# A casting transfer of GpSimd's in place of ScalarE's rounding, for the weight blocks of the second group's input projections

## The chip, the core and the metric

The kernel runs on one NeuronCore of a Trainium2 chip. Its engines are TensorE (PE in the profile; PEld is its weight load), VectorE (DVE), ScalarE (ACT), GpSimd (POOL) and SyncE (SP), which only issues transfers. Each has its own queue, worked off in order, and they meet at semaphores. The metric is the device time of one execution in microseconds (us); lower is better.

## What is computed

One layer of an encoder that mixes three groups of heads: a state-space scan in both directions (SSD), banded window attention, and cross-attention to a memory. It is applied to two requests with the same weights, 1024 rows and 256 rows, of width 2048, all in float32. Cut to what matters:

```
def layer(x, mem, ...):
    hn = rms_norm(x, norm_g)
    proj = hn @ w_in
    xbc, z_ssd, dt_raw, q, k, v, z_att, mq, z_mem = split_cols(proj, IN_SIZES)
    ...                       # convolution, scan, window attention, memory attention, gates
    return x + concatenate([o_ssd, o_att, o_mem], axis=-1) @ w_out
```

The two large products, by w_in and by w_out, are most of the arithmetic.

## The kernel before

The 1280 rows are ten tiles of 128; the kernel works in two groups of five tiles (640 rows). A float32 product is made of three products of float32r numbers, a form with fewer bits: each operand is split into a rounded part (h) and the rest (l = raw - h), and TensorE adds xH·wh, xH·wl and xL·wh in PSUM.

**The split of the weights.** The weights come in blocks of 128 x 512 (256 KB; those of kv are 128 x 288, 144 KB). SyncE loads a block into `wraw` (four buffers); `wsplit` (lines 204 to 208) rounds it into `wh` on ScalarE (line 206) and subtracts on VectorE into `wl` (line 207). `wh` and `wl` have three buffers each (WB = 3), so a buffer is free again when TensorE is done with the block three steps back:

```
a = A.activation(h, raw, AF.Copy)              # L206
b = V.tensor_sub(l, raw, h.bitcast(F32))       # L207
marks[:] = a.ins, b.ins
```

**The loops over blocks.** `block_tok` (line 234) walks over 16 blocks of 128 rows of the weights; per block it makes 5 tiles x 3 products of 512 (or 288) columns (lines 258 to 260), the last two blocks together, tile by tile, so that each tile's result can be taken away early. `block_feat` (line 268) walks over 8 blocks that each hold two times 128 rows of 256 columns, with the weights as the stationary side: 24 products of 320 columns per block (lines 293 to 295), the last two blocks together again. A third form, `block_pair` (line 1257), works on both groups' blocks at once by seven products in place of eight, in the first group's input blocks and at the end; it has its own call of `wsplit` and sums on GpSimd (line 1254).

**The order of the program.** After the memory's projections and the paired blocks come kv and z1 of the first group. Then come the second group's input blocks: x (six blocks of `block_feat`), kv, q, za (two), z0, z1, mq and zm (two). Blocks x, za and zm are made by `block_feat`, the others by `block_tok`. They hold 160 weight blocks: 48 in x, 16 in kv, 96 in the rest. Then the output blocks follow.

**The lanes.** Between the weight steps, two queues of generators ("lanes") advance the rest of the layer: `k_prep`, `attn`, `mem_attn` and others in lane 0, `dt_prep`, `ssd_up`, `ssd_down` in lane 1. `pump` (line 158) gives each lane so many steps per weight step by the table RATES. A lane step is recorded with `tc.issue_after` of the instructions in `marks`, those of the last split. Inside, the framework's scheduler sets the final order on each engine; `tc.high_priority` lets a split go ahead of work that was recorded earlier.

**What the lanes do on GpSimd.** `rsqrt` (lines 122 to 124) is two instructions there: `tensor_scalar` and a power. `k_prep` uses it on `kss` (line 520), a sum that VectorE makes at line 518 of squares that ScalarE makes at line 517; the result `krr` scales k. `mem_attn` does the same with `mss` (line 769) into `mr`, `attn` with `qss` into `qr`. Further there are small memsets (`lgw`, `mprw`, line 635) and copies (`lg`, line 683). Before the change no transfer is issued by GpSimd.

## Time and profile before

| | |
|---|---|
| median of 3 runs | 1782.76 us (1781.36 to 1782.76) |
| the profiled execution | 1782.24 us, its span 1780.5 us |
| granted TensorE clock | 1.00 |
| busy, TensorE / VectorE / ScalarE / GpSimd | 1766.1 / 1245.5 / 918.6 / 550.2 us |
| moved over the span | 168 GB/s |

[...] A row of a group reads: line, engine, operation, what it writes <- what it reads, count, then busy us and mean ns of one. A row of the timeline reads: start in us from the span's start, duration in us, engine, line, operation, shapes, count, and in brackets the idle time of that engine before it and who ended it.

### The profile page before, as it was taken

To read this page: it belongs to the slowest core of one execution; us is meant where nothing else is said; L and a number is where in the kernel's file an instruction comes from. 1 tells how busy PE (TensorE), PEld (TensorE's weight loads), DVE (VectorE), ACT (ScalarE), POOL (GpSimd) and SP (SyncE) were. 2 spreads that over 40 slices of the span, in tenths; PEclk is the share of its full clock that TensorE was granted. 3 is DMA by queue.
4 is the path that set the end of the run, shared out by engine and by line. 5 is a ranking of instruction groups with operands and counts; after the bars stand their busy time and mean duration, and the time that the engine had idled before them with its cause. 6 is when DMAs were issued, how large, how long until landed. Compare 5 with 4: busy or idle time off the path is not lost.

```text
span 1780.5 us, 31950 instructions
## 1 busy us (share of the span) xinstructions
PE 1766.1 (99%) x11046; PEld 1611.0 (90%) x11046; DVE 1245.5 (70%) x2348; ACT 918.6 (52%) x2049; POOL 550.2 (31%) x960
## 2 busy tenths in 40 slices
PE   9999999999999999999999999999999999999999
PEld 7889999999998999999889988887988888889999
DVE  5596788888868877877765676557777654766665
ACT  5555455554434766656464566544446633543332
POOL 0105899998810110011000100011100000058775
PEclk9999999999999999999999999999999999999999
DMA  8553454445446644453635655557777854644442
GB/s 302 192 182 124 136 153 148 142 142 164 123 145 202 196 131 135 149 166 101 193 121 179 197 151 161 170 161 248 223 239 230 255 188 141 221 145 143 148 142 78
DMA packets 208211, 301.16 MB, mean 169 GB/s; under 512 B 19569, under 2 KB 86193, under 8 KB 208049
## 3 DMA queue, kind: packets, MB, share of 16 engines
q1 hardware_dynamic: 207904, 299.06, 53.6%
q8 instruction: 87, 1.43, 0.3%
q14 instruction: 76, 0.61, 0.1%
q10 hardware_dynamic: 144, 0.06, 0.0%
HBM read 236.36 MB, written 62.69 MB: 168 GB/s over the span
## 4 chain that ended last, share of the span: by engine, by line
PE 88%; DVE 5%; issue 3%; DMA 2%; ACT 1%; POOL 1%; SPq 0%; POOLq 0%; DVEq 0%; ACTq 0%
PE acc L258 11%; PE acc L260 10%; PE acc L259 10%; PE acc L1288 7%; PE acc L1286 7%; PE acc L1287 7%; PE acc L293 5%; PE acc L295 5%; PE acc L294 5%; PE accm L1287 3%; PE accm L1286 3%; PE accm L1288 3%; PE po L723 1%; PE py L988 1%; DVE wl L207 1%
## 5 line engine op out<-in xcount | busy, mean ns | idle before, releaser
L207 DVE TENSOR_TENSOR wl<-wraw,wh 128x512 fp32r<-128x512 f32 (+1 forms) x480 | 347.4, 725 | 229.9 <-ACT wh L206 224.3
L206 ACT ACTIVATE wh<-wraw 128x512 fp32r<-128x512 f32 (+1 forms) x480 | 292.1, 613 | 297.1 <-PE acc L260 150.5
L258 PE MATMUL acc<-wh,xH 128*128 128x512 f32 (+1 forms) x1088 | 418.7, 385 | 0.2 <-DVE v_all L337 0.2
L260 PE MATMUL acc<-wh,xL 128*128 128x512 f32 (+1 forms) x1088 | 410.1, 377 | 0.0
L259 PE MATMUL acc<-wl,xH 128*128 128x512 f32 (+1 forms) x1088 | 409.7, 377 | 0.0
L258 PEld LDWEIGHTS acc<-wh,xH 128*128 128x128 f32 x1088 | 204.5, 188 | 36.9 <-issue 2.9
L260 PEld LDWEIGHTS acc<-wh,xL 128*128 128x128 f32 x1088 | 204.2, 188 | 37.0 <-issue 0.2
L259 PEld LDWEIGHTS acc<-wl,xH 128*128 128x128 f32 x1088 | 204.6, 188 | 35.3 <-issue 1.2
L293 PE MATMUL acc<-xH,wh 128*128 128x320 f32 x640 | 202.5, 316 | 0.2 <-DVE zs L309 0.2
L294 PE MATMUL acc<-xL,wh 128*128 128x320 f32 x640 | 198.9, 311 | 0.0
L295 PE MATMUL acc<-xH,wl 128*128 128x320 f32 x640 | 198.2, 310 | 0.0
L206 ACT ACTIVATE sh<-ws 128x384 fp32r<-128x384 f32 x176 | 91.2, 523 | 207.1 <-POOL ws L1254 103.4
L207 DVE TENSOR_TENSOR sl<-ws,sh 128x384 fp32r<-128x384 f32 x176 | 124.2, 709 | 95.8 <-ACT sh L206 94.0
L1254 POOL TENSOR_TENSOR ws<-wraw 128x128 f32<-128x128 f32 x176 | 111.1, 631 | 208.8 <-DMA wraw<-in_w_in_pairs_dram 93.6
L293 PEld LDWEIGHTS acc<-xH,wh 128*128 128x128 f32 x640 | 120.1, 188 | 2.7 <-issue 1.9
L294 PEld LDWEIGHTS acc<-xL,wh 128*128 128x128 f32 x640 | 120.2, 188 | 1.7 <-issue 1.4
L1254 POOL TENSOR_TENSOR ws<-wraw,ws 128x128 f32<-128x128 f32 x176 | 117.5, 667 | 13.8
L295 PEld LDWEIGHTS acc<-xH,wl 128*128 128x128 f32 x640 | 120.2, 188 | 0.7 <-issue 0.6
L1254 POOL TENSOR_TENSOR wraw<-wraw 128x128 f32<-128x128 f32 x176 | 112.6, 640 | 13.7
L1254 POOL TENSOR_TENSOR ws<-ws,wraw 128x128 f32<-128x128 f32 x176 | 116.2, 660 | 0.0
L635 POOL MEMSET lgw<- 128x1 f32 x40 | 3.9, 98 | 315.9 <-DVE lg L698 227.0
L362 DVE SCALAR_TENSOR_TENSOR c<-u,vec,c 128x638 f32<-128x638 f32 (+1 forms) x96 | 90.0, 939 | 9.1 <-ACT c L357 8.7
(439 smaller groups left out, 3951.0 us busy)
## 6 DMA issues: line engine op xcount, KB each, us to landing
wraw<-in_w_in_laid_dram SPq DMA_DIRECT2D x176, 256.0 KB, 2.9
wraw<-in_w_in_pairs_dram SPq DMA_DIRECT2D x112, 256.0 KB, 2.7
wraw<-in_w_out_laid_dram SPq DMA_DIRECT2D x64, 256.0 KB, 3.5
wraw<-in_w_out_pairs_dram SPq DMA_DIRECT2D x64, 256.0 KB, 2.7
rf<-ac SPq DMA_DIRECT2D x40, 256.0 KB, 4.1
rb<-ac SPq DMA_DIRECT2D x40, 256.0 KB, 4.8
wraw<-in_w_mem_laid_dram SPq DMA_DIRECT2D x32, 256.0 KB, 4.4
xst<-in_x_sample_dram SPq DMA_DIRECT2D x20, 256.0 KB, 5.7
```

The costliest lines, as they stand in the source:

```text
L206: a = A.activation(h, raw, AF.Copy)
L207: b = V.tensor_sub(l, raw, h.bitcast(F32))
L258: T.matmul(ps[t][:, :n], sh, h[:, :n], start=(k_ == 0), stop=False)
L259: T.matmul(ps[t][:, :n], sh, l[:, :n], start=False, stop=False)
L260: T.matmul(ps[t][:, :n], sl, h[:, :n], start=False, stop=(k_ == KT - 1))
L293: T.matmul(o, sh, cur["H", q][:, m, c], start=(k == 0), stop=False)
L294: T.matmul(o, sh, cur["L", q][:, m, c], start=False, stop=False)
L295: T.matmul(o, sl, cur["H", q][:, m, c], start=False, stop=(k == KT - 1))
L1254: G.tensor_tensor(out=o, in0=x, in1=y, op=op)
L1286: T.matmul(ps[p], h, xh, start=(k_ == 0), stop=False)
L1287: T.matmul(ps[p], h, xl, start=False, stop=False)
L1288: T.matmul(ps[p], l, xh, start=False, stop=(k_ == 7))
```

## The change

A second form of the split, `wsplit_loaded`, gets the source in DRAM too. GpSimd issues a transfer straight from there into `wh`; the buffer's type is float32r and the source's float32, so the transfer casts. VectorE's subtraction and SyncE's load of `wraw` stay, so a block is read from DRAM twice. `marks` holds the subtraction alone. `block_feat` always uses it; `block_tok` where `loaded` is set, which is so for kv, q, z0, z1 and mq of the second group, and not for the output blocks or those ahead of block x. `w_laid` hands on the source in place of a function that loads.

```
+    def wsplit_loaded(raw, h, l, src):
+
+        G.dma_start(h, src)
+        b = V.tensor_sub(l, raw, h.bitcast(F32))
+        marks[:] = [b.ins]
+
     def w_laid(src, n):
 
-        def load(k, raw):
-            S.dma_start(raw, src[k])
-        return load, n
+        return src, n
...
-    def block_tok(w, nt, evac, before_last=None, feats=range(KT), places=range(KT)):
-
-        load, n = w
+    def block_tok(w, nt, evac, before_last=None, feats=range(KT), places=range(KT), loaded=False):
+
+        src, n = w
...
-            load(feats[k], raw[:, :n])
+            S.dma_start(raw[:, :n], src[feats[k]])
...
-                wsplit(raw[:, :n], h[:, :n], l[:, :n])
+                if loaded:
+                    wsplit_loaded(raw[:, :n], h[:, :n], l[:, :n], src[feats[k]])
+                else:
+                    wsplit(raw[:, :n], h[:, :n], l[:, :n])
...
-                wsplit(raw, h.rearrange("p a c -> p (a c)"), l.rearrange("p a c -> p (a c)"))
+                wsplit_loaded(raw, h.rearrange("p a c -> p (a c)"), l.rearrange("p a c -> p (a c)"), src[kk])
...
-        run(block_tok(w, 5, evac), RATES[grp][name], after)
+        run(block_tok(w, 5, evac, loaded=name != "o"), RATES[grp][name], after)
...
-    run(block_tok(w_kv, 5, ev_dtkv(5)), RATES[1]["kv"], extra=lambda k: some_left() if left else None)
+    run(block_tok(w_kv, 5, ev_dtkv(5), loaded=True), RATES[1]["kv"], extra=lambda k: some_left() if left else None)
...
-    run(block_tok(w_in_rows("q"), 5, ev_raw(q_d, 5)), RATES[1]["q"], extra=when_done(2, lambda: queue(1, ssd_up, range(4, 8))))
+    run(block_tok(w_in_rows("q"), 5, ev_raw(q_d, 5), loaded=True), RATES[1]["q"], extra=when_done(2, lambda: queue(1, ssd_up, range(4, 8))))
```

Lines behind the new function have other numbers in the changed kernel: 212 is the transfer, 213 the subtraction, and 7 more than before farther down (516 becomes 523, and so on).

The scheduler puts the transfers between the lanes' instructions on GpSimd. At the start of block x, before, with the krr pairs of three `k_prep` steps:

```order
L123 TENSOR_SCALAR krr_7211<-kss_7207 128x2
L124 TENSOR_TENSOR krr_7211<-krr_7211,mhalf_87 128x2
L123 TENSOR_SCALAR krr_7299<-kss_7295 128x2
L124 TENSOR_TENSOR krr_7299<-krr_7299,mhalf_87 128x2
L123 TENSOR_SCALAR krr_7459<-kss_7455 128x2
L124 TENSOR_TENSOR krr_7459<-krr_7459,mhalf_87 128x2
L683 COPY lg_7986<-nsink_6131 128x2
```

The same place on GpSimd after, where wh_7249 is the first block of x0, wh_7304 the second and so on:

```order
L123 TENSOR_SCALAR krr_7211<-kss_7207 128x2
L124 TENSOR_TENSOR krr_7211<-krr_7211,mhalf_87 128x2
L212 DMA wh_7249<-in_w_in_laid_dram 128x512
L123 TENSOR_SCALAR krr_7299<-kss_7295 128x2
L124 TENSOR_TENSOR krr_7299<-krr_7299,mhalf_87 128x2
L212 DMA wh_7304<-in_w_in_laid_dram 128x512
L212 DMA wh_7348<-in_w_in_laid_dram 128x512
L690 COPY lg_7986<-nsink_6131 128x2
L212 DMA wh_7412<-in_w_in_laid_dram 128x512
L212 DMA wh_7464<-in_w_in_laid_dram 128x512
L123 TENSOR_SCALAR krr_7459<-kss_7455 128x2
L124 TENSOR_TENSOR krr_7459<-krr_7459,mhalf_87 128x2
```

The first transfer stands behind one krr pair, the second behind the next; the small copy has moved ahead of the last pair.

On VectorE at the same place, before, between the subtraction of x0's second block and what stands ahead of it (zs are the gates of the block before x0):

```order
L309 SCALAR_TENSOR_TENSOR zs_7171<-zs_7171,acc_6596 128x512
L194 SCALAR_TENSOR_TENSOR chd_7396<-chd_7396,vec_200,rbc_6320 128x640
L309 SCALAR_TENSOR_TENSOR zs_7181<-zs_7181,acc_6597 128x512
L309 SCALAR_TENSOR_TENSOR zs_7191<-zs_7191,acc_6598 128x512
L518 TENSOR_REDUCE kss_7295<-ksq_7296 128x2
L207 TENSOR_TENSOR wl_7305<-wraw_7302,wh_7304 128x512
```

And after, from the subtraction of the first block (wl_7250) to that of the second (wl_7305):

```order
L213 TENSOR_TENSOR wl_7250<-wraw_7247,wh_7249 128x512
L316 SCALAR_TENSOR_TENSOR zs_7171<-zs_7171,acc_6596 128x512
L983 COPY_PREDICATED rb_7054<-upper_6114,rf_7053 128x512
L525 TENSOR_REDUCE kss_7295<-ksq_7296 128x2
L316 SCALAR_TENSOR_TENSOR zs_7181<-zs_7181,acc_6597 128x512
L194 SCALAR_TENSOR_TENSOR chd_7396<-chd_7396,vec_200,rbc_6320 128x640
L316 SCALAR_TENSOR_TENSOR zs_7191<-zs_7191,acc_6598 128x512
L194 SCALAR_TENSOR_TENSOR chd_7445<-chd_7445,vec_200,rbc_6320 128x640
L957 COPY state_6124<-pst_7214 128x512
L316 SCALAR_TENSOR_TENSOR zs_7201<-zs_7201,acc_6599 128x512
L213 TENSOR_TENSOR wl_7305<-wraw_7302,wh_7304 128x512
```

The sum kss_7295, on which the second krr pair depends, stood two gates behind its neighbours and just ahead of the second subtraction; now it stands three instructions behind the first subtraction.

On GpSimd in block kv of the second group, before, with the mr pair and memsets of `mem_attn`:

```order
L635 MEMSET mprw_10361 128x1
L635 MEMSET mprw_10400 128x1
L123 TENSOR_SCALAR mr_10516<-mss_10514 128x4
L124 TENSOR_TENSOR mr_10516<-mr_10516,mhalf_87 128x4
L635 MEMSET mprw_10707 128x1
```

And after, where wh_10451 is the sixth block of kv and wh_10653 the eleventh:

```order
L212 DMA wh_10451<-in_w_in_laid_dram 128x288
L212 DMA wh_10488<-in_w_in_laid_dram 128x288
L212 DMA wh_10524<-in_w_in_laid_dram 128x288
L212 DMA wh_10567<-in_w_in_laid_dram 128x288
L212 DMA wh_10612<-in_w_in_laid_dram 128x288
L123 TENSOR_SCALAR mr_10516<-mss_10514 128x4
L124 TENSOR_TENSOR mr_10516<-mr_10516,mhalf_87 128x4
L212 DMA wh_10653<-in_w_in_laid_dram 128x288
L212 DMA wh_10683<-in_w_in_laid_dram 128x288
```

The mr pair stands between the transfers of the tenth and the eleventh block.

## The prediction

> **What bounds the kernel now.** I read the page first, then busy time in the stretch that the change touches, then what TensorE waits for there. The page:

> ```profile
> span 1780.5 us, 31950 instructions
> PE 1766.1 (99%) x11046; PEld 1611.0 (90%) x11046; DVE 1245.5 (70%) x2348; ACT 918.6 (52%) x2049; POOL 550.2 (31%) x960
> ```

> TensorE is busy for 1766.1 of 1780.5 us. It holds for the stretch of the second group's input blocks too. Here are the windows of blocks x (48 weight blocks), kv (16) and the rest (q, za, z0, z1, mq, zm: 96), then all three; columns: length, busy time of each engine, granted clock, share of the DMA engines, GB/s.

> ```profile
> 590.00:818.00 228.00, 224.99 (x1697) 215.85 (x1695) 173.75 (x386) 143.20 (x355) 20.21 (x47) 1.00 0.46 144
> 818.00:860.00 42.00, 40.70 (x311) 39.38 (x309) 34.26 (x72) 30.04 (x81) 6.18 (x8) 1.00 0.57 164
> 860.00:1312.00 452.00, 450.98 (x2801) 388.12 (x2801) 297.62 (x660) 240.44 (x601) 41.38 (x110) 1.00 0.58 183
> 590.00:1312.00 722.00, 716.68 (x4803) 643.36 (x4802) 505.63 (x1117) 413.68 (x1036) 67.78 (x165) 1.00 0.54 170
> ```

> In 722 us TensorE is idle for 5.3, at a clock of 1.00 throughout; ScalarE is busy for 57% of it and GpSimd for 9%. ScalarE is thus no bound, and the change can gain only what TensorE now loses to it. The waits of TensorE in that stretch (waiting, for whom: us in total, times, longest):

> ```profile
> PE psc L689 <- ACT qT L673: 2.4, 1, 2.4
> PE pmt L628 <- DVE mpr L805: 1.3, 1, 1.3
> PE psc L689 <- DVE nm L691: 0.7, 1, 0.7
> PE psc L689 <- DVE xs L909: 0.3, 1, 0.3
> PE acc L293 <- DVE zs L309: 0.2, 1, 0.2
> ```

> 4.9 us in all. None is a wait for a weight block: no row names wh or wl.

> **What goes: ScalarE's rounding.** Line 206 in the same three windows (ScalarE's busy time, count):

> ```profile
> 590.00:818.00 228.00, 30.72 (x50) 1.00 0.46 144
> 818.00:860.00 42.00, 6.30 (x14) 1.00 0.57 164
> 860.00:1312.00 452.00, 60.34 (x96) 1.00 0.58 183
> ```

> 97.4 us, for the 160 blocks that change, leave an engine with 308 idle us there. What can come out at the end is part of the 4.9 us of waits: the 2.4 us for qT is ScalarE's own, and ScalarE stands further back in the others. I take 2.5 us, between 0 and 4.9.

> **What comes: 160 transfers that GpSimd issues.** No transfer of GpSimd's is in this trace, so I bound them by SyncE's. The window's transfers from DRAM (KB each, median us from issue to landing), then SyncE's loads from the same tensor (how long its queue is held by one, min/median/max, and the landing of all):

> ```profile
> wraw<-in_w_in_laid_dram SPq DMA_DIRECT2D x139, 256.0 KB, 2.9
> rf<-ac SPq DMA_DIRECT2D x30, 256.0 KB, 3.5
> rb<-ac SPq DMA_DIRECT2D x28, 256.0 KB, 4.8
> wraw<-in_w_in_laid_dram SPq DMA_DIRECT2D x16, 144.0 KB, 2.5
> ...
> L275 SPq DMA_DIRECT2D wraw<-in_w_in_laid_dram x80: 327/333/949, 569.2 to 1286.4; - x80
> ...
> DMA to landing us min/median/max: 2.0/2.8/6.1
> ```

> The landing lies between 2.0 and 6.1 us. I take 4.0 for 256 KB, the middle of the rows of that size (2.9 to 4.8), since a cast and another issuer are hardly quicker than the plain load at 2.9, and 3.6 for 144 KB (0.4 less, as 2.5 is against 2.9). [...]

> What the issue takes of GpSimd lies between the 0.33 us of SyncE's queue and the 3.12 us of its longest instruction quoted below; at 1 us, 160 of them bring its 67.8 busy us to 228 of 722, which is hidden by idle time. The bytes are 144 blocks of 256 KB and 16 of 144 KB, 40 MB beside the 123 MB that the window moves at 170 GB/s: the DMA share goes from 0.54 to about 0.72. I cost that at nothing while a transfer has two steps of the weight loop to land in; without that cover it is the third rival.

> That cover: three wh buffers mean that a buffer is freed when the block three steps back is done, and its successor is needed two steps later. By the windows two steps are 2 x 228 / 48 = 9.5 us in x, 5.25 in kv and 9.4 in the rest. The new chain (landing, VectorE's subtraction of about 0.7, and some 0.7 of VectorE's queue) is 5.4 us, and 3.6 + 0.45 + 0.5 = 4.55 in kv. So it fits on average, with 4 us to spare in x and the rest and 0.7 in kv. I book 1 us for kv's shorter steps, and nothing for the others.

> **What waits behind what.** GpSimd runs in order, and its lane work now stands between the transfers. Place one is the start of block x0. The rows of before, on GpSimd, VectorE, ScalarE and TensorE:

> ```profile
> 583.99 0.69 POOL L124 TENSOR_TENSOR krr<-krr,mhalf 128x2 f32<-128x2 f32 x1
> 592.40 0.56 POOL L123 TENSOR_SCALAR krr<-kss 128x2 f32<-128x2 f32 x1 [7.71 <-DVE kss L518]
> 593.04 0.70 POOL L124 TENSOR_TENSOR krr<-krr,mhalf 128x2 f32<-128x2 f32 x1
> ...
> 585.73 0.69 DVE L207 TENSOR_TENSOR wl<-wraw,wh 128x512 fp32r<-128x512 f32 x1
> 586.53 0.74 DVE L976 COPY_PREDICATED rb<-upper,rf 128x512 f32<-128x512 uint32 x1
> 587.17 0.66 DVE L309 SCALAR_TENSOR_TENSOR zs<-zs,acc 128x512 f32<-128x512 f32 x1
> 592.03 0.28 DVE L518 TENSOR_REDUCE kss<-ksq 128x2 f32<-128x128 f32 x1
> ...
> 589.55 0.38 PE L293 MATMUL acc<-xH,wh 128*128 128x320 f32 x1
> 593.59 0.31 PE L293 MATMUL acc<-xH,wh 128*128 128x320 f32 x1
> ```

> x0's first block is used from 589.55, its second from 593.59. In the new order the first transfer stands behind the krr pair that ends at 584.7: it lands at 588.7, the subtraction ends at 589.4, just in time. The second stands behind the next pair, whose kss now follows that subtraction on VectorE, after a zs and an rb: 589.4 + 0.66 + 0.74 + 0.28 = 591.1 at the earliest, and 592.3 as before. The pair then ends between 592.4 and 593.7; the transfer lands between 596.4 and 597.7, and the subtraction ends between 597.1 and 598.4. TensorE stands still for 3.5 to 4.8 us: I take 4.

> Place two is in kv, where the transfer of the eleventh block stands behind the mr pair:

> ```profile
> 842.45 0.57 POOL L123 TENSOR_SCALAR mr<-mss 128x4 f32<-128x4 f32 x1 [13.75 <-DVE mss L769]
> 843.10 3.12 POOL L124 TENSOR_TENSOR mr<-mr,mhalf 128x4 f32<-128x4 f32 x1
> ...
> 843.68 0.45 DVE L207 TENSOR_TENSOR wl<-wraw,wh 128x288 fp32r<-128x288 f32 x1
> ...
> 846.92 0.29 PE L258 MATMUL acc<-wh,xH 128*128 128x288 f32 x1
> ...
> L124 POOL TENSOR_TENSOR mr<-mr,mhalf 128x4 f32<-128x4 f32 x10 | 12.5, 1255 | 0.8
> ```

> Its first product came at 846.92. Behind the pair's end at 846.2 it would land at 849.8 and be split by 850.3, 3.4 us late; if the power takes its mean of 1.26 us in place of 3.12, 1.5 us late. I take 3, nearer to the row of this very place. Elsewhere the lane instructions ahead of a transfer ended before its buffer was free in before, or so little later that the 4 us cover it. The other way round, lane work queued behind a waiting transfer runs later by at most a few us; VectorE, which waits for it, has 30% of the window idle. Where the subtraction waits for a transfer, VectorE's lane work stands behind it, as it stood behind ScalarE's rounding.

> **The sum.** + 4 (x0) + 3 (mr) + 1 (kv) - 2.5 (ScalarE) = + 5.5 us. The profiled execution took 1782.24 us (span 1780.5), 0.5 below the median of 1782.76; 1782.24 + 5.5 = 1787.7 us, slower by 0.3%. A measurement of this kernel can tell some 0.2%, 3.6 us, from no change.

> **The rivals.** First, faster: relief decides. If krr's pair of x0 ends by 588.9 (593.59 less 4.0 and 0.7), since an emptier ScalarE brings its inputs sooner, the second transfer is in time, and likewise at mr; then all 4.9 us of waits may go: 1777.3 us. For it, every wait of the list lies downstream of ScalarE or VectorE; against it, kss stands behind the first block's subtraction, which itself waits for a landing. Chance 0.22.

> Second, no difference: the landing is nearer to the plain load's 2.9, or the krr pair a little earlier, and the stalls of 2 to 6 us pay for what relief brings: within 1778.7 and 1785.8 us. Chance 0.27.

> [...] Chance 0.15. [...]

> That the change doesn't do what it says is excluded by the order: the 160 transfers stand on GpSimd and as many roundings are gone from ScalarE.

> **How the numbers follow.** The forecast has 0.36, and with the third rival slower has 0.51; the same 0.27, faster 0.22. The range goes from the faster rival's 1777 to 1803, which leaves out the dearer part of the third rival and of the faster one a tail, some 0.18 together.

> **What would show it.** Right: TensorE's waits list wl at x0's second block and at kv's eleventh, with GpSimd's transfers issued just behind krr and mr, and landings near 4 us; the qT wait is gone. Wrong: TensorE's idle time between 590 and 1312 stays at 5 us or falls, or the stalls are spread over all blocks and landings are 5 us or more; or TensorE waits for lane results that GpSimd brings late, which I cost at nothing.

## The result, and the profile after

The changed kernel takes 1881.41 us (median of 4 runs, 1876.43 to 1887.43), the kernel before, run beside it, 1782.76 us (1781.36 to 1785.56): a ratio of 1.0558, 95% interval 1.0539 to 1.0578. That is 98.7 us more, where 5.5 were forecast; the direction was right, the size wrong by a factor of 18, and the time lies far above the range. The head of the changed kernel's page:

```profile
span 1885.6 us, 31992 instructions
PE 1806.5 (96%) x11046; PEld 1638.3 (87%) x11046; DVE 1245.4 (66%) x2348; ACT 837.3 (44%) x1889; POOL 634.4 (34%) x1120
```

The profiled execution is the slowest of the four (1887.43 us), 105.2 us above that of the kernel before. All of this is lost in the stretch that was changed. Here it is in the same three parts and as a whole (blocks x, kv, the rest), and behind it, from the kernel before, the whole stretch with the same blocks:

```profile
592.00:856.00 264.00, 240.79 (x1709) 228.67 (x1708) 174.38 (x388) 124.98 (x321) 46.22 (x97) 0.94 0.61 175
856.00:910.00 54.00, 48.27 (x362) 45.54 (x362) 36.96 (x84) 21.42 (x57) 14.86 (x25) 0.97 0.67 179
910.00:1425.00 515.00, 473.64 (x2790) 402.16 (x2789) 300.38 (x658) 187.84 (x501) 92.14 (x202) 0.96 0.69 209
592.00:1425.00 833.00, 762.69 (x4857) 676.37 (x4856) 511.71 (x1127) 334.24 (x876) 153.22 (x324) 0.96 0.66 196
```

```profile
590.00:1318.00 728.00, 722.68 (x4843) 648.88 (x4841) 508.77 (x1123) 417.39 (x1045) 68.60 (x165) 1.00 0.54 169
```

The stretch is 105 us longer. TensorE's idle time goes from 5.3 us (728.00 less 722.68) to 70.3, 65 more; its busy time grows by 40.0 with the same products (a few more lie inside the window's edges), most of it because the granted clock is 0.96 in place of 1.00. VectorE has the same work (511.7 and 508.8 us). By the first products of the blocks the loss is 35 us in x, 7 in kv and 61 in the rest: it is everywhere. What TensorE waits for:

```profile
PE psc L696 <- ACT qT L680: 11.0, 5, 4.0
PE acc L300 <- DMA wh<-in_w_in_laid_dram: 7.9, 2, 4.0
PE psc L696 <- DVE nm L698: 5.0, 3, 2.5
PE acc L265 <- DMA wh<-in_w_in_laid_dram: 4.9, 3, 2.5
PE ppt L635 <- DVE lg L705: 4.8, 2, 3.9
PE pxs L914 <- DMA xc<-xbc_d: 4.2, 1, 4.2
```

Waits for a transferred weight block are 12.8 us (7.9 and 4.9, five of them). Nearly all the rest is spread over a long list of results and loads of the lanes, led by qT, nm, lg and xc. So what is late is mostly not the weights but the other work. The landings are no worse than forecast in the median, though the longest takes 7.6 us (KB, median; then GpSimd's time for one issue in ns, min/median/max, and all landings):

```profile
wh<-in_w_in_laid_dram POOLq DMA_DIRECT2D x144, 256.0 KB, 3.6
wh<-in_w_in_laid_dram POOLq DMA_DIRECT2D x16, 144.0 KB, 2.6
...
L212 POOL DMA_DIRECT2D wh<-in_w_in_laid_dram x160: 527/528/806, 587.8 to 1409.0; - x160
DMA to landing us min/median/max: 2.4/3.5/7.6
```

A hint why the lanes are late is that VectorE stands still ahead of its subtractions. The group of the subtractions in the stretch, before (two of the next block are in it) and after; behind the bar busy time and mean, then VectorE's idle time just ahead of them:

```profile
L207 DVE TENSOR_TENSOR wl<-wraw,wh 128x512 fp32r<-128x512 f32 (+1 forms) x162 | 107.7, 665 | 93.3 <-ACT wh L206 92.4
```

```profile
L213 DVE TENSOR_TENSOR wl<-wraw,wh 128x512 fp32r<-128x512 f32 (+1 forms) x160 | 106.5, 666 | 203.4 <-DMA wh<-in_w_in_laid_dram 101.2 <-issue 43.3 <-PE py L995 17.3
```

93.3 us became 203.4: 110 us more. That VectorE idles some 102 us more in all in a stretch that is 105 us longer follows from its nearly equal work; what the rows tell is that all of it lies ahead of the subtractions. They don't tell cause from effect; the experiments do. One place of the changed kernel in order of time, in block z0, shows how such a stop can reach TensorE (start, duration, engine, line; in brackets the idle time ahead of it and what ended it):

```profile
1086.11 0.17 DVE L704 RECIPROCAL den<-den 128x2 f32<-128x2 f32 x1 [1.87 <-ACT lg L702]
...
1089.40 0.69 DVE L213 TENSOR_TENSOR wl<-wraw,wh 128x512 fp32r<-128x512 f32 x1 [3.12 <-DMA wh<-in_w_in_laid_dram]
1090.01 0.75 DVE L705 TENSOR_SCALAR lg<-lg,den 128x384 f32<-128x384 f32 x2
...
1090.48 0.74 PE L635 MATMUL ppt<-identr,lgw 128*128 128x128 f32 x4 [3.94 <-DVE lg L705]
```

At 1086.28 `den` is done, and the scaling of `lg` (line 705) could start. Next in VectorE's queue is a subtraction, whose block lands 3.12 us later. `lg` stands behind it and, though ready, does not start in these 3.12 us, and TensorE, which has come to the transposes of `lg`, stands still for 3.94 us, though the block itself is in no hurry (in the median of the 160, a subtraction ends 5.0 us ahead of its block's first product). At 1088.60 the clock then falls to half for 6.83 us.

### The profile page after: what moved, and what is told of

It is laid out like the page before. It is cut to its first block, busy times and chain, and to the rows that moved or that the text cites. A ratio compares the mean times of both kernels' runs of the same rounds, so it can differ in the third digit from the quotient of the medians.

```text
span 1885.6 us, 31992 instructions
## 1 busy us (share of the span) xinstructions
PE 1806.5 (96%) x11046; PEld 1638.3 (87%) x11046; DVE 1245.4 (66%) x2348; ACT 837.3 (44%) x1889; POOL 634.4 (34%) x1120
## 5 line engine op out<-in xcount | busy, mean ns | idle before, releaser
L266 PE MATMUL acc<-wl,xH 128*128 128x512 f32 (+1 forms) x1088 | 414.0, 381 | 1.0 <-DVE wl L213 0.8
L207 DVE TENSOR_TENSOR wl<-wraw,wh 128x512 fp32r<-128x512 f32 (+1 forms) x320 | 239.3, 750 | 133.8 <-ACT wh L206 131.6
L206 ACT ACTIVATE wh<-wraw 128x512 fp32r<-128x512 f32 (+1 forms) x320 | 194.6, 615 | 166.1 <-PE acc L267 91.4
L213 DVE TENSOR_TENSOR wl<-wraw,wh 128x512 fp32r<-128x512 f32 (+1 forms) x160 | 106.5, 666 | 203.4 <-DMA wh<-in_w_in_laid_dram 101.2
L212 POOL DMA_DIRECT2D wh<-in_w_in_laid_dram x160 | 88.0, 550 | 423.1 <-PE acc L302 123.0
L300 PE MATMUL acc<-xH,wh 128*128 128x320 f32 x640 | 210.7, 329 | 8.4 <-DMA wh<-in_w_in_laid_dram 7.9
L302 PE MATMUL acc<-xH,wl 128*128 128x320 f32 x640 | 205.3, 321 | 0.0
L301 PE MATMUL acc<-xL,wh 128*128 128x320 f32 x640 | 204.5, 320 | 0.0
L207 DVE TENSOR_TENSOR sl<-ws,sh 128x384 fp32r<-128x384 f32 x176 | 124.5, 710 | 99.7 <-ACT sh L206 96.3
L300 PEld LDWEIGHTS acc<-xH,wh 128*128 128x128 f32 x640 | 126.4, 198 | 12.2 <-DMA wh<-in_w_in_laid_dram 8.4
L301 PEld LDWEIGHTS acc<-xL,wh 128*128 128x128 f32 x640 | 126.2, 197 | 2.0 <-issue 1.7
L302 PEld LDWEIGHTS acc<-xH,wl 128*128 128x128 f32 x640 | 125.4, 196 | 1.4 <-DVE wl L213 0.8
## 6 DMA issues: line engine op xcount, KB each, us to landing
wraw<-in_w_in_laid_dram SPq DMA_DIRECT2D x176, 256.0 KB, 2.9
wh<-in_w_in_laid_dram POOLq DMA_DIRECT2D x144, 256.0 KB, 3.6
wraw<-in_w_in_pairs_dram SPq DMA_DIRECT2D x112, 256.0 KB, 2.8
wraw<-in_w_out_laid_dram SPq DMA_DIRECT2D x64, 256.0 KB, 3.4
wraw<-in_w_out_pairs_dram SPq DMA_DIRECT2D x64, 256.0 KB, 2.7
rf<-ac SPq DMA_DIRECT2D x40, 256.0 KB, 4.1
rb<-ac SPq DMA_DIRECT2D x40, 256.0 KB, 5.9
wraw<-in_w_mem_laid_dram SPq DMA_DIRECT2D x32, 256.0 KB, 4.4
```

Of the source, the lines that this page charges most:

```text
L212: G.dma_start(h, src)
L266: T.matmul(ps[t][:, :n], sh, l[:, :n], start=False, stop=False)
L300: T.matmul(o, sh, cur["H", q][:, m, c], start=(k == 0), stop=False)
L301: T.matmul(o, sh, cur["L", q][:, m, c], start=False, stop=False)
L302: T.matmul(o, sl, cur["H", q][:, m, c], start=False, stop=(k == KT - 1))
```

## The experiments

There are eighteen kernels, each run beside the kernel before; "+x" is the difference of the medians. Theory A: VectorE stands still for landings, and the lane work queued behind is late. B: GpSimd's lane work stands behind its transfers. C: the 40 MB more of traffic slow the lanes' loads.

**1. The subtraction doesn't wait (sub_apart).** VectorE multiplies the raw block by itself, so it no longer reads the transferred block.

```diff
         G.dma_start(h, src)
-        b = V.tensor_sub(l, raw, h.bitcast(F32))
+        b = V.tensor_mul(l, raw, raw)
```

> The changed kernel, but VectorE's 160 subtractions are products of the raw block with itself: the same engine, shape and place, no reading of the transferred block (the low part of the weights is wrong for it). VectorE no longer waits for a landing; TensorE still does. Theory A (VectorE stands still for the landings, its lane work queued behind comes late to TensorE): VectorE's idle time before wl falls from 203 to under 100 us and the time to 1785 to 1800 us, with the two stalls for weight blocks (4 and 3 us) left. Theory B (GpSimd's lane work stands behind transfers that wait for their buffers) and theory C (40 MB more traffic slow the lanes' loads): 1860 to 1885 us, since transfers, order on GpSimd and traffic are the same.

1816.88 us, ratio 1.0186 (1.0164 to 1.0207): +33.6. VectorE's idle time ahead of these instructions is back at 99.9 us, and none of it is for a weight block's landing:

```profile
L213 DVE TENSOR_TENSOR wl<-wraw 128x512 fp32r<-128x512 f32 (+1 forms) x159 | 105.8, 666 | 99.9 <-PE acc L266 60.3 <-PE acc L302 38.2 <-DMA xc<-xbc_d 0.8
```

With the same transfers, 65 of the 98.7 us are gone: A, as far as it goes, but the time is 16.9 us above the top of A's range, so something else takes part.

**2. Traffic without waits (spare_transfers, then spare_pinned).**

```diff
-        G.dma_start(h, src)
+        a = A.activation(h, raw, AF.Copy)
         b = V.tensor_sub(l, raw, h.bitcast(F32))
-        marks[:] = [b.ins]
+        marks[:] = a.ins, b.ins
+        s = dr.tile([P, 512], F32R, tag="spare", name="spare", bufs=4)[:, :raw.shape[-1]]
+        G.dma_start(s, src)
```

> ScalarE's rounding as in the kernel before, and beside it the 160 casting transfers of GpSimd's into four spare blocks in DRAM that nothing reads: the traffic and the issues of the change without its waits. Theory C (traffic): over 1830 us, with rf and rb landing as late as in the changed kernel (3.9 and 6.0 us). Theories A and B: 1781 to 1790 us, no more than a few us for GpSimd's 160 issues of 0.55 us.

1860.41 us, +77.1, and a miss as an experiment: transfers that wait for nothing were put at the very start of the program. There they took the DMA engines from the first loads; the first 50 us, with TensorE busy for 29.33 (48.70 in before) and a DMA share of 0.95 (0.89):

```profile
0.00:50.00 50.00, 29.33 (x78) 20.70 (x79) 11.89 (x21) 12.78 (x19) 21.84 (x49) 0.76 0.95 326
```

Block x0 starts 79 us late (668.6 for 589.6), and from there to the stretch's last product it takes 726.6 us, for 727.1 in before. The second kernel adds an edge in the order behind the subtraction (no wait), and its spare blocks are rows of 2 KB with gaps between them:

```diff
-        s = dr.tile([P, 512], F32R, tag="spare", name="spare", bufs=4)[:, :raw.shape[-1]]
-        G.dma_start(s, src)
+        s = dr.tile([P, 1024], F32R, tag="spare", name="spare", bufs=4)[:, :raw.shape[-1]]
+        g = G.dma_start(s, src)
+        tc.add_manual_dep(g.ins, b.ins.name, BEHIND, reason="place in the order")
```

> ScalarE's rounding as in the kernel before, with the 160 casting transfers to spare blocks in DRAM in rows of 2 KB, each now held in GpSimd's order at the place where the change has it, but waiting for no buffer. Theory C (traffic beside the lanes' loads): the stretch of the second group's input blocks grows from 729 us to over 745 us and the time to over 1800 us. Theories A and B: 1781 to 1788 us, the stretch within 5 us of 729.

1807.10 us, ratio 1.0151 (1.0132 to 1.0169): +25.9. The stretch with its DMA share of 0.72, and VectorE's idle time ahead of wl, which is that of before:

```profile
588.00:1343.00 755.00, 734.69 (x4856) 658.86 (x4855) 510.57 (x1125) 416.18 (x1046) 152.09 (x323) 0.99 0.72 215
```

```profile
L214 DVE TENSOR_TENSOR wl<-wraw,wh 128x512 fp32r<-128x512 f32 (+1 forms) x159 | 105.5, 664 | 89.8 <-ACT wh L213 85.7 <-DMA wraw<-in_w_in_laid_dram 3.3
```

So C is real: this traffic by itself costs 26 us, where the prediction had nothing. TensorE's new waits are few and again for the lanes:

```profile
PE psc L700 <- ACT qT L684: 5.4, 3, 3.7
PE pxs L918 <- DMA xc<-xbc_d: 2.7, 1, 2.7
PE pq L682 <- DVE xs L920: 2.7, 1, 2.7
```

These transfers write to DRAM and not to SBUF, and press harder on the other loads: SyncE's wraw lands in 3.9 us here (median over the whole program, 256 KB), 2.9 in the changed kernel and in before. So 26 us is rather an upper figure for the change's own traffic.

**3. GpSimd's queue (lanes_off_pool, both_off, gate).** First the lanes' arithmetic goes to VectorE, then the same together with edit 1:

```diff
-        G.tensor_scalar(out=dst, in0=src, scalar1=scale, scalar2=EPS, op0=ALU.mult, op1=ALU.add)
-        G.tensor_tensor(out=dst, in0=dst, in1=mhalf[:, :n], op=ALU.pow)
+        V.tensor_scalar(out=dst, in0=src, scalar1=scale, scalar2=EPS, op0=ALU.mult, op1=ALU.add)
+        V.reciprocal(out=dst, in_=dst)
...
-        G.memset(w.bitcast(F32)[(slice(None),) + tuple(slice(n - 1, n) for n in shape)], 0.0)
+        V.memset(w.bitcast(F32)[(slice(None),) + tuple(slice(n - 1, n) for n in shape)], 0.0)
```

> The changed kernel with all arithmetic of the lanes moved from GpSimd to VectorE (the power of -0.5 becomes a reciprocal there, so the square root is left out): GpSimd has only its transfers. Theory B: the lane work is no longer behind a waiting transfer, and the time falls to 1783 to 1820 us. Theory A: VectorE still waits for every landing and has some 30 us more work in the stretch: 1875 to 1900 us. Theory C: as A.

> The two edits together: the product that doesn't read the transferred block in place of the subtraction (low parts wrong), and the lanes' arithmetic on VectorE (the square root left out). By themselves they gave back 64.5 and 29.7 of the 98.7 us. If theories A (VectorE behind landings) and B (lane work behind GpSimd's transfers) are both true and apart from each other, the sum is 94 us and the time 1785 to 1795 us. If the traffic (C) or the landings that TensorE itself waits for cost something of their own, it stays at 1805 to 1815 us, no lower than 10 us under the first edit alone.

1851.67 us (+68.4), outside the ranges of A and of B, and 1813.75 us (+32.6). By the first alone B seemed worth 30 us; but beside edit 1 it gives 1 us (33.6 against 32.6). The third kernel puts B by itself into the kernel before, with a memset of 0.1 us in the transfer's place and with its wait (`read_by` holds TensorE's last product with each block; WRITTEN makes a wait, BEHIND in the other kernels an order alone):

```diff
+        g = G.memset(gate_, 0.0)
+        tc.add_manual_dep(g.ins, read_by[split[0] - 3].ins.name, WRITTEN, reason="its buffer's last reader")
```

> ScalarE's rounding as in the kernel before, and on GpSimd, at the places of the 160 transfers, a memset of one column that waits until TensorE has read the wh buffer's last block, as the transfer does: theory B alone, with no landing and no traffic. Theory B: 1800 to 1820 us (what is left where VectorE doesn't read the transferred block is 34 us), with TensorE's waits on qT as in the changed kernel. If B is wrong and those 34 us are landings or traffic: 1781 to 1790 us.

1781.09 us, ratio 1.0001 (0.9992 to 1.0011): nothing, though GpSimd stands still in these waits for over 400 us of the stretch:

```profile
POOL gate__200 L218 <- PE acc L273: 209.2, 72, 8.1
POOL gate__200 L218 <- PE acc L309: 205.6, 61, 8.0
```

B falls as a cause of its own. What lanes_off_pool gives back, it gives only where VectorE waits too. Of its two changes, transfers issued a little sooner (0.33 us in the mean behind the buffer's release, for 0.74) and lane chains without the way over GpSimd, the runs don't tell which.

**4. VectorE's wait without traffic (tiny4, tiny2, tiny1).** ScalarE rounds as before; GpSimd issues four, two or one transfers of 512 bytes when the wh buffer is free, and the subtraction waits for the last:

```diff
         a = A.activation(h, raw, AF.Copy)
+        for i in range(4):
+            f, g = g if i else None, G.dma_start(gate_[:, i:i + 1].bitcast(F32R), src[:, i:i + 1])
...
         b = V.tensor_sub(l, raw, h.bitcast(F32))
+        tc.add_manual_dep(b.ins, g.ins.name, WRITTEN, reason="the last small transfer")
```

> ScalarE's rounding as in the kernel before; at each of the 160 places GpSimd issues four transfers of 512 bytes (the first waits until the wh buffer is free, as the change's transfer does), and VectorE's subtraction waits for the last of them: four issues of 0.5 us and a landing near 2 us, about the 4.1 us from issue to landing of the changed kernel, with next to no traffic. Theory A alone: VectorE's idle time before wl rises from 93 to some 200 us and the time to 1840 to 1860 us (98.7 us less the 26 that the traffic cost by itself). If VectorE's wait is harmless: 1781 to 1790 us, and what the first edits gave back came from somewhere else.

> As the run with four small transfers, but with two: from the buffer's release to the subtraction some 4.7 us, about the 4.9 us of the changed kernel, and no traffic. If wait and traffic add up, the wait alone gives 98.7 less 26, 1845 to 1860 us, with VectorE idle for some 160 to 200 us before wl. If the wait alone makes the whole loss and the traffic is hidden behind it: 1870 to 1885 us. If only the longer wait of the four did harm: under 1820 us.

> The same with one small transfer: some 4.1 us from release to subtraction (1.0 with ScalarE's rounding). If the loss is in proportion to the wait beyond 1.0 us (100 us for 5.6 us more): 3.1 us more, some 55 us, 1835 us. If there is a length up to which VectorE's free time takes it: 1781 to 1800 us.

1881.63, 1864.53 and 1871.22 us: +99.9, +83.1 and +89.8, ratios 1.0570 (1.0541 to 1.0599), 1.0464 (1.0432 to 1.0495) and 1.0497 (1.0481 to 1.0513). From the end of TensorE's last product with the block three before to the start of the subtraction (median of the 160, worked out from the starts and ends in the trace) it is 1.05 us in the kernel before, 4.88 in the changed one, and 6.75, 5.48 and 5.07 here. So one or two transfers of half a kilobyte at each of the 160 places, at about the changed kernel's length of wait, cost 90 and 83 us; with four it is +99.9, 22 us above the expected range. The one transfer lands in 3.0 us, each of the four of tiny4 in 2.8 (medians; near 2 was expected), and VectorE's idle time is that of the changed kernel:

```profile
gate__200<-in_w_in_laid_dram POOLq DMA_DIRECT2D x160, 0.5 KB, 3.0
...
L223 DVE TENSOR_TENSOR wl<-wraw,wh 128x512 fp32r<-128x512 f32 (+1 forms) x160 | 106.5, 666 | 206.6 <-DMA gate__200<-in_w_in_laid_dram 130.3 <-issue 19.0 <-ACT wh L216 11.5
```

A fifth of TensorE's waits there, 13.0 of 64 us, is for the subtraction's own result, the rest nearly all for the lanes:

```profile
PE acc L278 <- DVE wl L223: 6.6, 5, 2.3
PE acc L315 <- DVE wl L223: 6.4, 4, 1.8
```

A is shown from both sides: without the wait 65 us are gone, and the wait alone makes 83 to 90 us. The traffic alone makes up to 26, both together 98.7. They don't add up; that a lane that waits for VectorE loses nothing more by a late load is my reading of it, not shown. My 55 us for tiny1 (a loss in proportion to the wait) was too low: its wait is as long as the changed kernel's, 1.3 us of it ahead of the issue.

**5. From what length on (wait_two, wait_four).** As in 4, with two or four GpSimd instructions in place of transfers:

```diff
-            f, g = g if i else None, G.dma_start(gate_[:, i:i + 1].bitcast(F32R), src[:, i:i + 1])
+            g = G.tensor_scalar(out=gate_, in0=gate_, scalar1=1.0, scalar2=0.0, op0=ALU.mult, op1=ALU.add)
```

> ScalarE's rounding as before; at each of the 160 places two GpSimd instructions of 0.6 us, the first waiting for the buffer's release, and VectorE's subtraction waits for the second: some 1.7 us from release to subtraction in place of 1.0. In proportion (90 us for 4.0 us more) some 16 us: 1797 us. If VectorE's free time takes such a wait: 1781 to 1787 us.

> The same with four such instructions: some 2.9 us from release to subtraction. In proportion some 43 us: 1825 us. If the harm comes from transfers and not from VectorE's wait as such: 1781 to 1787 us. If waits up to half a step of 4.7 us are taken by free time: under 1795 us.

1788.93 us, +6.8 (ratio 1.0036, 1.0023 to 1.0048) and 1806.97 us, +24.8 (1.0133, 1.0118 to 1.0148). The waits came out shorter than meant (1.17 and 1.69 us), so neither the one forecast nor the other is tested as it was written; the idle time ahead of wl is the better measure:

```profile
L221 DVE TENSOR_TENSOR wl<-wraw,wh 128x512 fp32r<-128x512 f32 (+1 forms) x159 | 105.8, 665 | 105.6 <-POOL gate__200 L218 77.4 <-ACT wh L216 14.3 <-DMA xc<-xbc_d 4.9
```

```profile
L221 DVE TENSOR_TENSOR wl<-wraw,wh 128x512 fp32r<-128x512 f32 (+1 forms) x159 | 106.1, 668 | 136.7 <-POOL gate__200 L218 115.2 <-ACT sq L668 8.7 <-POOL lgw L653 3.5
```

93.3, 105.6, 136.7 and 206.6 us of idle VectorE go with +0, +6.8, +24.8 and +89.8: 12 us more cost 6.8, 43 more 24.8, 113 more 89.8. tiny2, with 192.8 us idle, has +83.1. No transfer is needed for it, and no free allowance is seen down to these 12 us: over half of each us that VectorE stands still there more than before reaches the end.

**6. Mending A (wh4_raw3, late_sub, sub_on_pool).** Earlier transfers, a later subtraction, and the subtraction on another engine:

```diff
-CH, WB, RB, WA, WBB = 4, 3, 4, 5, 4
+CH, WB, RB, WA, WBB = 4, 3, 3, 5, 4
...
-                h = wp.tile([P, 512], F32R, tag="wh", name="wh", bufs=WB)
+                h = wp.tile([P, 512], F32R, tag="wh", name="wh", bufs=4)
```

```diff
         b = V.tensor_sub(l, raw, h.bitcast(F32))
+        tc.add_manual_dep(b.ins, read_by[split[0] - 2].ins.name, BEHIND, reason="place in the order")
```

```diff
-        b = V.tensor_sub(l, raw, h.bitcast(F32))
+        b = G.tensor_sub(l, raw, h.bitcast(F32))
```

> The changed kernel with four wh buffers in place of three and three raw buffers in place of four (SBUF holds no more): each casting transfer may be issued a step, some 4.7 us, earlier. Theory A: nearly every landing is over when VectorE comes to its subtraction, and the time falls to 1785 to 1815 us. Theory B: GpSimd's transfers wait less for their buffers, so a part of it, 1820 to 1850 us. Theory C: no change, 1870 to 1890 us; the kernel with fewer raw buffers may also hold SyncE's queue longer, which would add to each.

> The changed kernel, with each subtraction placed in VectorE's order no earlier than TensorE's last product of the block two before it (order alone, no wait): lane work goes ahead of it while the transfer lands. Theory A: VectorE's idle time before wl falls from 203 to some 120 us and the time to 1830 to 1860 us; TensorE may then wait for wl itself, a few us more than now. Theories B and C: 1870 to 1890 us.

> The changed kernel with the 160 subtractions on GpSimd, right behind their transfers, in place of VectorE: the wait for the landing and the lane work that is queued behind it part. A wait on GpSimd was harmless by itself. Theory A: the lanes are in time, and the time falls to that of the traffic and TensorE's own waits, 1805 to 1840 us (GpSimd's subtraction is slower, 1.5 to 2.5 us by its 0.6 us for 128 columns, so some waits of TensorE for wl come in). If the loss lies in the late weight blocks or in their landing: 1880 us or more.

wh4_raw3: 1872.82 us, +89.5, a miss. The edit costs 20.6 us before the stretch begins (x0 starts at 610.2), presumably by the three raw buffers; from there to the stretch's last product it takes 793 us, 37 less than in the changed kernel. Waits for landings fell from 101.2 to 27.7 us, but VectorE still idles for 156.3 ahead of wl: the subtraction keeps its early place in the queue, and now waits for a wl buffer.

```profile
L213 DVE TENSOR_TENSOR wl<-wraw,wh 128x512 fp32r<-128x512 f32 (+1 forms) x159 | 105.8, 666 | 156.3 <-PE acc L266 38.0 <-issue 33.3 <-PE acc L302 28.7
```

late_sub: 1856.05 us, +74.9: order alone gives 24 us back, as A has it, though the idle time ahead of wl fell only to 164.8 us, not to 120. sub_on_pool: 1967.67 us, +186.2, and my expectation was wrong. GpSimd's next transfer now stands behind the subtraction that waits for the last landing, and is issued 3.3 us behind its buffer's release in place of 0.4 (medians). TensorE now waits 52 us for wh and wl themselves:

```profile
L213 POOL TENSOR_TENSOR wl<-wraw,wh 128x512 fp32r<-128x512 f32 (+1 forms) x160 | 208.1, 1302 | 463.2 <-DMA wh<-in_w_in_laid_dram 229.1 <-issue 97.4 <-PE acc L302 28.5
```

A wait on GpSimd's queue that was harmless ahead of a memset in the gate kernel goes with the largest loss of all where the next transfers are queued behind it. No version here beats the kernel before.

**7. What relief there was (short_round).**

```diff
-        a = A.activation(h, raw, AF.Copy)
+        G.memset(h[:, 32:].bitcast(F32), 0.0)
+        a = A.activation(h[:, :32], raw[:, :32], AF.Copy)
```

> The kernel before, with ScalarE rounding 32 of the 512 columns of each of the 160 blocks and GpSimd filling the others with zeros (the rounded part is left out there): ScalarE is relieved of nearly all that the change takes from it, with no transfer. By the prediction's step 2.5 us are to be had, between 0 and 4.9: 1776 to 1783 us. All theories agree here; it prices what the change could have gained at the most.

1784.53 us, ratio 1.0012 (1.0002 to 1.0022), +2.8: no gain. The edit isn't clean, since VectorE now waits for GpSimd's zeros (103.6 us idle ahead of wl for 93.3, some 6 us by experiment 5), which can hide a small one. But TensorE's wait for qT, which I had put down to ScalarE's load, is still there at the same place (2.4 in before):

```profile
PE psc L697 <- ACT qT L681: 2.1, 1, 2.1
```

**8. What a stall costs (stall_short, stall_long, stall_nine).** In the kernel before, the first product of one weight block in ten waits for one, four or nine GpSimd instructions that start when the block before is done.

```diff
+            for i in range(9):
+                g = G.tensor_scalar(out=gate_, in0=gate_, scalar1=1.0, scalar2=0.0, op0=ALU.mult, op1=ALU.add)
...
+            tc.add_manual_dep(first.ins, g.ins.name, WRITTEN, reason="held up")
```

> The kernel before, with TensorE held up at 16 places of the stretch (one in ten weight blocks): its first product of the block waits for one GpSimd instruction of some 0.6 us that starts when the block before is done; about 1.0 us each. If a stall costs its own length: some 16 us, 1797 us; the granted clock stays at 1.00.

> The same 16 places with four such GpSimd instructions in a row, about 2.8 us each. If a stall costs its own length: 45 us, 1826 us. If a stall that fills over half of one of the 3.41 us cells of the clock's grid is followed by half clock for 3.41 or 6.83 us, as in the changed kernel: 1.7 to 3.4 us more for each, 1850 to 1880 us, with some 16 dips in the clock's record.

> The kernel before with TensorE held up by a chain of nine GpSimd instructions in place of four (which held it for 1.4 us at the most, at 7 places): some 3 us more at each of 7 to 16 places. At its own length only: 25 to 55 us, 1807 to 1835 us. With half clock for 3.41 or 6.83 us behind every stall that fills over 1.7 us of a cell: 12 to 50 us more, and as many dips in the clock's record as there are such stalls.

+3.8, +14.0 and +40.1 us (1785.53, 1795.66 and 1821.53); in each the hold-up fell on 14 places. At many of them TensorE had lane products to do meanwhile, so the stalls were fewer and shorter than meant. In stall_short none is over 0.6 us, and the clock has no dip in the stretch. In stall_long they are 12.2 us, one of 5.0 us among them, and behind that one is the only dip, of 6.83 us. The third has the most:

```profile
PE acc L318 <- POOL gate__200 L227: 17.5, 6, 5.7
PE acc L282 <- POOL gate__200 L227: 6.8, 4, 3.3
...
PE acc L318 <- POOL lgw L660: 2.1, 1, 2.1
```

These are 26.4 us of stalls; the last row is one too, with a lane's memset put at the end of GpSimd's chain. In all, TensorE's idle time in the stretch grows by 27.1 us and its busy time by 14.6. The granted clock has eight dips to 0.50 (seven of 3.41 us, one of 6.83). TensorE is busy for 27.8 of these 30.7 us, and half of that, 13.9 us, explains the second part. So a stall is paid at its own length, and the longer ones a second time by the clock: 26.4 and 13.9 are 40.3 us, of 40.1 measured.

## Why the prediction was wrong

**The step that failed** is the sentence "Where the subtraction waits for a transfer, VectorE's lane work stands behind it, as it stood behind ScalarE's rounding", with the lines ahead of it that cost such lateness at nothing because VectorE "has 30% of the window idle". The mechanism was named and then priced at zero. Behind ScalarE's rounding the subtraction started some 1 us after the buffer's release, behind a transfer 4.9 us after it (medians); here, idle time of VectorE in the mean did not help the instruction that stands behind a waiting one. Experiment 4 puts this at 83 to 90 us by itself, and experiments 1 and 5 agree.

**Point by point.**
- Relief of ScalarE, -2.5 us: not seen; the qT wait that it was to remove stays with ScalarE relieved (2.1 us, experiment 7), and in the changed kernel the waits for qT are 11.0 us.
- The landing, 4.0 and 3.6 us: 3.6 and 2.6.
- GpSimd's issue, 1 us: 0.53, and hidden, as forecast.
- The DMA engines' share, 0.72, at nothing: 0.72 in spare_pinned, at 26 us (0.66 in the longer stretch of the changed kernel). This is the second failing term.
- The cover of two steps: TensorE indeed waits for transferred blocks only five times, 12.8 us, where 8 were forecast (x0, mr and kv). The chain to a weight block was counted rightly; the chain that grew was another.
- Place one, x0's second block, 3.5 to 4.8 us: right in place and cause, a transfer behind the krr pair. The length of 3.93 us is partly luck: the pair ended earlier than forecast against the block's start (1.9 us behind it, for 2.9 to 4.2), the landing took 6.5 us in place of 4.0, and the first product waits for wh alone, without the 0.7 us of the subtraction. On GpSimd, VectorE and TensorE of the changed kernel:

```profile
593.75 0.19 POOL L123 TENSOR_SCALAR krr<-kss 128x2 f32<-128x2 f32 x1 [5.12 <-DVE kss L525]
594.02 0.72 POOL L124 TENSOR_TENSOR krr<-krr,mhalf 128x2 f32<-128x2 f32 x1
594.71 1.15 POOL L212 DMA_DIRECT2D wh<-in_w_in_laid_dram  x2
...
601.21 0.64 PE L300 MATMUL acc<-xH,wh 128*128 128x320 f32 x1 [3.93 <-DMA wh<-in_w_in_laid_dram]
```

- Its price was short of the clock's share. The time cells of 3.41 us around it (TensorE's busy time is the second figure, the granted clock the third from the end):

```profile
597.09:600.50 3.41, 0.19 (x2) 0.00 (x0) 0.54 (x1) 1.32 (x5) 0.53 (x1) 1.00 0.77 235
600.50:607.33 6.83, 6.12 (x22) 5.90 (x23) 6.01 (x13) 3.05 (x7) 0.00 (x0) 0.50 0.75 226
```

Half of the 6.12 busy us is 3.1 more: x0 grew by 7.3 us (31.4 to 38.7), not 4.
- Place two, kv's block behind the mr pair, 3 us: right, 2.51 (a landing of 3.0 us behind GpSimd's power instruction of 2.17), and a dip of 3.41 us behind it.

```profile
884.03 2.17 POOL L124 TENSOR_TENSOR mr<-mr,mhalf 128x4 f32<-128x4 f32 x1
...
886.18 1.67 POOL L212 DMA_DIRECT2D wh<-in_w_in_laid_dram  x3
...
889.20 0.40 PE L265 MATMUL acc<-wh,xH 128*128 128x288 f32 x1 [2.51 <-DMA wh<-in_w_in_laid_dram]
```

- The clock, taken as 1.00 throughout: in the stretch it dips fifteen times (nine of 3.41 us, six of 6.83: 71.7 us at half speed). TensorE is busy for 62.3 of these, and half of that, 31 us, is the bulk of the 40.0 us that it is busy longer.
- The third rival, much slower by landings of 6.1 us (the longest of SyncE's in the kernel before), from which the range has its upper end: the time went its way and beyond, but no run shows such landings of wh as the rule. In the changed kernel the median is 3.5 us and the longest 7.6, and an issue takes 0.53 (0.81 at the most). At 256 KB the medians are 3.6 us there, and 3.7 to 4.0 in sub_apart, lanes_off_pool, both_off, wh4_raw3 and late_sub.
- The prediction's last sentence named the sign that came: "TensorE waits for lane results". Only that they come late by VectorE, not by GpSimd.

**What stays open.** Without A, 33 us are left (experiment 1), of which traffic makes up to 26. In the kernels in which ScalarE has lost its rounding it stands long for the lanes' loads (63.9 and 46.4 us for rf and rb in the changed kernel, 75.8 and 36.0 in sub_apart; 3.1 for rf before, 12.7 in tiny1, where it still rounds). TensorE's largest wait in sub_apart, 10.6 of 27.9 us, is for qT, which ScalarE makes:

```profile
PE psc L696 <- ACT qT L680: 10.6, 5, 4.2
```

In the changed kernel qT once stands behind such a load:

```profile
643.30 0.69 ACT L978 ACTIVATE rb<-rb,wj_all 128x128 f32<-128x128 f32 x2 [4.84 <-DMA rb<-ac]
643.90 0.57 ACT L680 ACTIVATE qT<-pq 128x512 fp32r<-128x512 f32 x1
...
644.53 0.39 PE L696 MATMUL psc<-kT,qT 128*128 128x256 f32 x1 [4.00 <-ACT qT L680]
```

Whether the order on ScalarE, which no longer has a rounding in each step to stand behind, costs something of its own was not tried. Nor was the nearest mending of A: the lane steps are put behind the subtraction by `marks`, and no kernel leaves it out of `marks` to let them pass.

## What to carry to other kernels

When a step's input comes from a transfer in place of an engine, ask what stands behind the waiting instruction on its queue and who needs that, and price it by the idle time that the wait adds on that queue, not by the engine's mean idle share. Here 0.55 to 0.8 of this added idle time came out at the end, although the engine had 30% idle and the step's own result was nearly always early enough. The wait's growth times the number of places would have been too much: 3.8 us at 160 places is some 610 us, of which 110 became idle time. In this kernel, with TensorE 99% busy, many lanes were only just in time, so late ones were paid for, and again by the clock. Try the wait by itself (a transfer of a few bytes) before the whole change: it shows the loss without the traffic.

## What the runs showed of the hardware

```profile
719.96:723.38 3.42, 1.71 (x14) 1.71 (x15) 2.99 (x7) 1.61 (x5) 0.00 (x0) 1.00 0.24 90
723.38:726.79 3.41, 3.41 (x15) 3.41 (x14) 3.31 (x7) 0.56 (x2) 0.52 (x2) 0.50 0.24 77
```

- A transfer of GpSimd's of 512 bytes lands in 3.0 us in tiny1, one of 256 KB in 3.6 in the changed kernel (medians): at this size most of it doesn't go with the bytes.
- The 160 subtractions (144 of 128 x 512 numbers, 16 of 128 x 288) take GpSimd 1.30 us in the mean (sub_on_pool), VectorE 0.67 (the changed kernel).
